# Unread f32 products in the norm gaps and the router, and layer 1's modulation sums moved beside layer 0's feed-forward part

## The chip, the cores and the metric

The kernel runs on one core of a Trainium2 chip. The metric is the device time of one execution in microseconds (us): the median of three runs of the kernel before is 2724.13 us (2723.62 to 2729.8). The engines named below are TensorE (PE, the matrix products; PEld is its weight load), VectorE (DVE), ScalarE (ACT), GpSimd (POOL) and SyncE (SP, which issues the weight loads).

## The reference

Two blocks of two layers each, one after the other, on 256 tokens of width 1024, in float32. Cut to what matters here:

```
# first block, layers l = 0, 1: x (256 tokens) and, in layer 0, ctx (256 more)
mod = silu(c) @ w_mod[l] + b_mod[l]           # six vectors of 1024: shift, scale, gate, twice
h1  = modulate(rmsnorm(h, norm1_g[l]), shift1, scale1)
h   = h + gate1 * (mixing_layer(h1 @ w_in[l]) @ w_out[l])
h2  = modulate(rmsnorm(h, norm2_g[l]), shift2, scale2)
h   = h + gate2 * conv_ffn(h2)

def conv_ffn(h, w_up, conv_w, conv_b, w_down):
    u = h @ w_up                              # 5632 columns
    u = three-tap convolution of u along the tokens
    a, b = split(u, 2)
    return (silu(a) * b) @ w_down

# second block
h = h + even_mix(rmsnorm(h)) ; h = h + swiglu(rmsnorm(h))
h = h + odd_mix(rmsnorm(h))  ; h = h + moe_swiglu(rmsnorm(h))   # a router picks experts
out = rmsnorm(h)
```

The modulation vectors of layer 1 depend on the conditioning input alone, so they can be computed at any time before layer 1's first norm. (Layer 1 needs them for both streams in its first norm, and for the main stream alone elsewhere.)

## The kernel before

Feature rows lie on the 128 partitions and tokens along the free axis, 512 columns in layer 0 (both streams), 256 elsewhere. An f32 product of accuracy is made of three (`mm3`, L519 to L521): high part times high part, low times high, high times low, where the high part is a rounded copy made by ScalarE (`wh`, L488) and the low part the residual made by VectorE (`wl`, L489). Weights come through `load_f` (L514, issued by SP) into a ring of raw tiles `wf`; with three slots in the ring during the feed-forward part, a load waits until the tile three loads earlier is read out.

The stages in order: start and layer 0's mix (to 336 us), the gap of its second norm (to 348), layer 0's feed-forward part (348 to 745), the gap of layer 1's first norm (745 to 752), layer 1's mix (to 951), the second norm and feed-forward part (to 1143), the leave step (1144 to 1153), the second block's first layer (mix to 1358, norm gap, swiglu to 1551), its second layer (norm gap, mix to 1690), the router (1690 to 1697), the experts (to 2708), and the last norm.

A norm (`rstd`, L555) squares tiles of h on ScalarE (L563), adds them on GpSimd (L568) except for the last two, takes column sums with one-column products (L574), a root on ScalarE (L576), a reciprocal on VectorE (L577), and spreads the result over the partitions with `spread` (L605). `modnorm` (L633, L639, L640) then makes the high and low parts `ah`, `al` that the next matmuls need. `first_rstd` (L608) does the same for the very first norm; `leave` (L1151) for the end of the first block, with two norms in one.

The feed-forward part runs in two halves of eleven steps j. In each j two products `up` (a, then b; 24 records each) are followed by the convolution (`conv`: L1092 on ScalarE, L1095 and L1096 on VectorE), the multiply L1070, and the split into `gh`, `gl`. Three ups are started ahead, side by side. After eleven j come the down products.

Layer 1's modulation vectors are made by `mods_v` (L686) on VectorE: a chunk is 384 columns of `w_mod`, loaded in two tiles of 768 KB; for each stream one first product (L698) and seven adding ones (L700), then three one-column products on TensorE (L705) and an add (L708). Six chunks have two streams, ten have one. It is a generator that stops twice in each chunk. `tick` (L712) advances the first unfinished generator in `self.fill`. Before, `fill` held the rest of layer 0's own vectors (`m0`) and then layer 1's (`m1`); it was ticked from places in the mixes, and once in each j of layer 0's feed-forward part, which spread layer 1's sixteen chunks thus: one two-stream chunk in layer 0's mix, five two-stream and six one-stream chunks in layer 0's feed-forward part, four one-stream chunks in layer 1's mix. Instructions are placed by a scheduler that hoists what it can, so the order on an engine isn't that of the text.

Of the kernel before, what the change touches and what calls it, by code (L numbers as in the profile page):

```python
# [16 lines left out]
P = 128  # L17
D = 1024
KT = 8
S = 256  # L20
# [409 lines left out]
class Build:  # L430
# [36 lines left out]
    def load_consts(self, pool, g):  # L467
        n = sum(_CP[x].shape[1] for x in GROUPS[g])
        t = self.mk(pool, [P, n], F32, "c" + g)
        (self.nc.sync if g == "A" else self.nc.gpsimd).dma_start(out=t, in_=self.I["consts" + g])  # L470
        o = 0
        for x in GROUPS[g]:
            w = _CP[x].shape[1]
            self.cs[x] = t[:, o:o + w]
            o += w
        return t
# [75 lines left out]
    def rstd(self, src, kts, n, ones, eps, lead=None):  # L552


        nc = self.nc  # L555
        nt = n // P
        lead = kts - 2 if lead is None else lead
        ps = self.smps()
        r = self.mk(self.wk, [P, 8], F32, "rs", 1)
        total = self.mk(self.wk, [P, n], F32, "ssq", 1) if lead else None  # L560
        for k in range(kts):
            sq = self.t2k()
            nc.scalar.activation(sq[:, :n], src[:, k, :n], AF.Square)  # L563
            if k == (kts - 3 if lead else 1):
                nc.scalar.activation(r[:, 4:5], sq[:, :1], AF.Sqrt)
            if k < lead:
                if k:
                    nc.gpsimd.tensor_tensor(total, total, sq[:, :n], op=OP.add)  # L568
                else:
                    nc.gpsimd.tensor_copy(total, sq[:, :n])  # L570
                continue
            for i, x in enumerate((total, sq) if lead and k == lead else (sq,)):
                for t in range(nt):
                    nc.tensor.matmul(ps[:, t:t + 1], x[:, t * P:t * P + P], ones[:, :1],  # L574
                                     start=k == lead and i + t == 0, stop=k == kts - 1 and t == nt - 1)
        nc.scalar.activation(r[:, :nt], ps[:, :nt], AF.Sqrt, bias=eps)  # L576
        nc.vector.reciprocal(r[:, :nt], r[:, :nt])  # L577
        out = self.smps()
        self.spread(out, r[:, :nt])
        return out  # L580

    def head_rstd(self, sq, n, eps, floor=None):

# [24 lines left out]
    def first_rstd(self, h):  # L608

        nc = self.nc  # L610
        ps = self.smps()
        for k in range(KT):
            sq = self.t2k()
            nc.scalar.activation(sq, h[:, k], AF.Square)
            nc.tensor.matmul(ps, self.c("mean"), sq, start=k == 0, stop=k == KT - 1)
        r = self.mk(self.wk, [P, 512], F32, "ssq", 1)
        nc.scalar.activation(r, ps, AF.Sqrt, bias=self.eps)
        nc.vector.reciprocal(r, r)
        return r
# [292 lines left out]
    def layer_a(self, l):  # L912
# [14 lines left out]
        rs = self.first_rstd(h) if l == 0 else self.rstd(h, KT, N, self.c("mean"), self.eps)  # L927
        if l == 0:
            self.m0 = self.mods(0, ((6, 7, 8, 9), (10, 11, 12, 13), (14, 15)))
            self.m1 = [self.mods_v(1, list(range(6)), 2), self.mods_v(1, list(range(6, 16)), 1)]  # L930
            self.fill = [self.m0] + self.m1

            keep = self.wp, self.wbufs
            sx = ExitStack()
            self.weights(sx, "wpS", (8, 1), 1536, 768)
            start = self.wp, self.wbufs
            m = self.mods(0, MODS_FIRST)
            for _ in MODS_FIRST[0]:
                next(m)
            self.wp, self.wbufs = keep  # L940
            first = [self.load_w(wq[i], KT, P) for i in lead]
            self.wp, self.wbufs = start
            self.drain(m)
            sx.close()
            self.wp, self.wbufs = keep
            self.load_consts(self.bp, "A")
            gs, sh = self.gains(l, 0, "norm1_g", ((0, 3), (3, KT)))
            m = self.m0
        else:
            self.drain(self.m1[0])  # L950
            m = self.m1[1]
            first = [self.load_w(wq[i], KT, P) for i in lead]
            gs, sh = self.gains(l, 0, "norm1_g")
# [103 lines left out]
        gh = self.mk(fp, [P, HT, NX], F32R, "gh")  # L1057
        gl = self.mk(fp, [P, HT, NX], F32R, "gl")

        def up(i):  # L1060
            ps = first.pop(0) if first else self.fm(self.load_w(w_up[i], KT, P), 0, act, 0, NX)
            return self.conv(l, ps, i, ns)

        for half in range(2):
            for f in range(HT):
                j = half * HT + f
                a = up(j)
                nc.scalar.activation(a[:, :NX], a[:, :NX], AF.Silu)
                b = up(NF + j)
                nc.vector.tensor_tensor(b[:, :NX], a[:, :NX], b[:, :NX], op=OP.mult)  # L1070
                if l == 0:
                    self.tick()
                self.split(gh[:, f], gl[:, f], b[:, :NX])
            for ft in range(0, KT, 2):

                ws = [self.load_w(I["w_down"][l, ft + i][:, half * HT:(half + 1) * HT], HT, P) for i in range(2)]
                ps = self.side(ws, (gh, gl), (NX, NX)) if ft == 0 else (self.fm(w, 0, (gh, gl), 0, NX) for w in ws)
                for i, p in enumerate(ps):
                    self.residual(l, ft + i, p, 40, ns)
        self.tap(f"hff{l}", h)  # L1080
        fx.close()
        rs = self.leave() if l else None
# [68 lines left out]
    def leave(self):  # L1151

        nc = self.nc
        ps = self.smps()
        r = self.mk(self.wk, [P, 8], F32, "rs", 1)
        total = self.mk(self.wk, [P, 2 * S], F32, "ssq", 1)
        h = self.h
        for k in range(KT):
            sq = self.t2k()
            hk = self.h[:, k, :S]  # L1160
            nc.scalar.activation(sq[:, :S], hk, AF.Square)
            nc.scalar.activation(sq[:, S:], hk, AF.Square, scale=self.v("final_g", k))
            if k == KT - 3:
                nc.scalar.activation(r[:, 4:5], sq[:, :1], AF.Sqrt)
            if k == 0:
                nc.gpsimd.tensor_copy(total, sq)
            elif k < KT - 2:
                nc.gpsimd.tensor_tensor(total, total, sq, op=OP.add)
            for x in {KT - 2: (total, sq), KT - 1: (sq,)}.get(k, ()):
                for t in range(4):  # L1170
                    nc.tensor.matmul(ps[:, t:t + 1], x[:, t * P:t * P + P], self.c("mean")[:, :1],
                                     start=x is total and t == 0, stop=k == KT - 1 and t == 3)
        r1, r2 = r[:, :2], r[:, 2:4]
        nc.scalar.activation(r1, ps[:, :2], AF.Sqrt, bias=self.eps)
        nc.vector.reciprocal(r1, r1)
        out = self.smps()
        self.spread(out, r1)
        nc.vector.tensor_tensor(r2, r1, r1, op=OP.mult)
        nc.vector.tensor_tensor(r2, r2, ps[:, 2:4], op=OP.mult)
        nc.scalar.activation(r2, r2, AF.Sqrt, bias=self.eps)  # L1180
        nc.vector.reciprocal(r2, r2)
        self.spread(out[:, S:], r2)

        def enter(k):
            nc.vector.scalar_tensor_tensor(self.hb[:, k], h[:, k, :S], self.v("final_g", k), out[:, :S],
                                           op0=OP.mult, op1=OP.mult)

        return out[:, S:], enter
# [427 lines left out]
    def moe(self, sums, copies):  # L1616
# [17 lines left out]
        sel = self.mk(mp, [P, 2, E], F32, "sel")  # L1634
# [4 lines left out]
        rs = self.mk(rp, [P, 2], F32, "rst")  # L1639
# [4 lines left out]
        for tt in range(2):  # L1644
            nc.vector.tensor_copy(lr[:, tt], sums[2 + tt][:, :E])
        nc.vector.reciprocal(rs, rs)

        for tt, sl, ps in copies:
            nc.scalar.activation(th[:, tt, sl], ps, AF.Copy, scale=rs[:, tt:tt + 1])
# [13 lines left out]
        ps = self.smps()  # L1663
# [16 lines left out]
        for tt, sl, pt in copies:  # L1680
            nc.vector.scalar_tensor_tensor(tl[:, tt, sl], pt, rs[:, tt:tt + 1], th[:, tt, sl].bitcast(F32),
                                           op0=OP.mult, op1=OP.subtract)
        cnt = self.mk(mp, [P, 1], F32, "cnt")
        cnti = self.mk(mp, [P, 1], mybir.dt.int32, "cnti")
        nc.vector.tensor_reduce(cnt, cps[:, :E], axis=AX.X, op=OP.max)
# [301 lines left out]
```

## Time and profile before

| | us |
|---|---|
| median of three runs (lowest, highest) | 2724.13 (2723.62, 2729.8) |
| the profiled execution, time | 2726.23 |
| its span | 2724.5 |
| TensorE busy | 2627.1 (96%) |
| VectorE busy | 1969.7 (72%) |
| ScalarE busy | 1566.6 (57%) |
| GpSimd busy | 179.8 (7%) |
[...]

The span is the time from the first to the last instruction of the profiled execution; its time has 1.7 us more around it. [...] A busy share is an average over stages: where TensorE's is near 1, another engine's work costs nothing as long as TensorE never waits for it.

### The profile page before, as it was taken

What the parts mean: (1) busy time and instruction counts of PE and PEld (TensorE: products, weight loads), DVE (VectorE), ACT (ScalarE), POOL (GpSimd) and SP (SyncE); (2) the same over time, 40 slices, a digit from 0 to 9 for tenths busy, and PEclk for the clock granted to TensorE, in tenths of its full rate; (3) what the DMA queues carried; (4) which work ended last, traced back from release to release, by engine and by line L of the source; (5) the groups of instructions that cost most, each with busy time, mean ns of one, the idle gap of its engine ahead of it and who ended that gap; (6) DMA issues with size and microseconds to landing.
All of it is one profiled execution on the core that took longest, in us unless ns stands there. A gap on an engine that the chain in (4) does not pass through costs nothing.

```text
span 2724.5 us, 39224 instructions
## 1 busy us (share of the span) xinstructions
PE 2627.1 (96%) x14886; PEld 2186.7 (80%) x14886; DVE 1969.7 (72%) x2975; ACT 1566.6 (57%) x2363; POOL 179.8 (7%) x212
## 2 busy tenths in 40 slices
PE   7999989999998999999999999999999999999998
PEld 4755678888877799998899988888887787788776
DVE  4245678467366787775665468999989888888886
ACT  4334434234244665564444465877777777777775
POOL 0120200000112200222100100000000000000000
PEclk9999989999999999999999999999999999999999
DMA  7344234344233255530256445899999999999992
GB/s 276 120 140 159 70 114 149 128 147 157 97 126 118 94 181 182 192 123 24 93 178 208 162 166 214 329 366 352 328 356 348 356 339 362 344 360 334 362 347 101
DMA packets 116178, 585.92 MB, mean 215 GB/s; under 512 B 19792, under 2 KB 24416, under 8 KB 71056
## 3 DMA queue, kind: packets, MB, share of 16 engines
q1 hardware_dynamic: 113744, 576.19, 58.8%
q0 software_dynamic: 2240, 7.16, 1.1%
q8 instruction: 119, 1.95, 0.3%
q14 instruction: 75, 0.61, 0.1%
HBM read 581.82 MB, written 1.47 MB: 214 GB/s over the span
## 4 chain that ended last, share of the span: by engine, by line
PE 87%; DVE 5%; DMA 3%; ACT 2%; issue 1%; POOL 0%; SPq 0%; DVEq 0%; ACTq 0%; POOLq 0%
PE mm L519 21%; PE mm L520 21%; PE mm L521 21%; PE dn L520 4%; PE dn L519 4%; PE dn L521 4%; PE sm L166 1%; DVE wl L489 1%; DMA wf<-w_mod 1%; PE sm L1764 1%; DVE m L700 1%; PE sm L772 1%; DMA wf<-w_qkg 1%; PE sm L908 1%; PE sm L1714 1%
## 5 line engine op out<-in xcount | busy, mean ns | idle before, releaser
L489 DVE TENSOR_TENSOR wl<-wf,wh 128x1024 fp32r<-128x1024 f32 (+3 forms) x1178 | 1210.4, 1056 | 357.0 <-ACT wh L488 352.3
L488 ACT CAST wh<-wf 128x1024 fp32r<-128x1024 f32 (+3 forms) x1178 | 1044.2, 912 | 595.3 <-PE mm L520 319.1
L519 PE MATMUL mm<-ah,wh 128*128 128x256 f32 (+1 forms) x1768 | 577.1, 330 | 15.5 <-ACT ah L639 4.0
L521 PE MATMUL mm<-ah,wl 128*128 128x256 f32 (+1 forms) x1768 | 576.6, 327 | 1.7 <-DVE wl L489 1.6
L520 PE MATMUL mm<-al,wh 128*128 128x256 f32 (+1 forms) x1768 | 574.3, 325 | 1.1 <-DVE al L637 1.1
L519 PEld LDWEIGHTS mm<-ah,wh 128*128 128x128 f32 x1768 | 338.9, 193 | 58.3 <-issue 8.5
L521 PEld LDWEIGHTS mm<-ah,wl 128*128 128x128 f32 x1768 | 340.4, 193 | 36.7 <-issue 5.3
L520 PEld LDWEIGHTS mm<-al,wh 128*128 128x128 f32 x1768 | 340.7, 193 | 31.0 <-issue 2.6
L520 PE MATMUL mm<-wl,xh 128*128 128x512 f32 x896 | 357.6, 399 | 2.0 <-DVE wl L489 2.0
L519 PE MATMUL mm<-wh,xh 128*128 128x512 f32 x896 | 355.8, 397 | 0.0
L521 PE MATMUL mm<-wh,xl 128*128 128x512 f32 x896 | 353.3, 395 | 0.0
L520 PEld LDWEIGHTS mm<-wl,xh 128*128 128x128 f32 x896 | 168.4, 188 | 52.0 <-DVE wl L489 13.1
L519 PEld LDWEIGHTS mm<-wh,xh 128*128 128x128 f32 x896 | 168.4, 188 | 38.9
L521 PEld LDWEIGHTS mm<-wh,xl 128*128 128x128 f32 x896 | 168.2, 188 | 37.9
L521 PE MATMUL dn<-wh,eal 128*128 128x512 f32 x448 | 180.7, 403 | 0.0
L520 PE MATMUL dn<-wl,eah 128*128 128x512 f32 x448 | 177.8, 397 | 0.0
L519 PE MATMUL mm<-gh,wh 128*128 128x256 f32 (+1 forms) x528 | 167.9, 318 | 0.0
L521 PE MATMUL mm<-gh,wl 128*128 128x256 f32 (+1 forms) x528 | 167.9, 318 | 0.0
L520 PE MATMUL mm<-gl,wh 128*128 128x256 f32 (+1 forms) x528 | 167.9, 318 | 0.0
L519 PE MATMUL dn<-wh,eah 128*128 128x512 f32 x448 | 157.6, 396 | 0.0
L520 PEld LDWEIGHTS mm<-gl,wh 128*128 128x128 f32 x528 | 99.8, 189 | 8.1
L521 PEld LDWEIGHTS mm<-gh,wl 128*128 128x128 f32 x528 | 99.8, 189 | 8.0
(502 smaller groups left out, 3320.1 us busy)
## 6 DMA issues: line engine op xcount, KB each, us to landing
wf<-moe_wg SPq DMA_DIRECT2D x112, 1024.0 KB, 6.9
wf<-moe_wu SPq DMA_DIRECT2D x112, 1024.0 KB, 6.9
wf<-moe_wd SPq DMA_DIRECT2D x112, 1024.0 KB, 6.3
wf<-w_mod SPq DMA_DIRECT2D x64, 768.0 KB, 4.5
wf<-w_up SPq DMA_DIRECT2D x88, 512.0 KB, 3.5
wf<-w_down SPq DMA_DIRECT2D x32, 704.0 KB, 4.1
wf<-w_qkg SPq DMA_DIRECT2D x30, 512.0 KB, 4.7
wf<-ffn_wg SPq DMA_DIRECT2D x22, 512.0 KB, 4.2
```

The source lines that it names most:

```text
L166: self.nc.tensor.matmul(o, l, r, start=True, stop=True)
L488: nc.scalar.copy(dh, src)
L489: nc.vector.tensor_tensor(dl, src, dh.bitcast(F32), op=OP.subtract)
L519: nc.tensor.matmul(out, lh, rh, start=first, stop=False)
L520: nc.tensor.matmul(out, lh, rl, start=False, stop=False)
L521: nc.tensor.matmul(out, ll, rh, start=False, stop=last)
L700: nc.vector.scalar_tensor_tensor(acc[s], w3[:, k - k0], c, acc[s], op0=OP.mult, op1=OP.add)
L772: nc.tensor.transpose(pt[:, k * P:k * P + P], pr[:, k * P:k * P + P], self.c("ident"))
L908: nc.tensor.matmul(ops[rows, s * S:s * S + S], nav[:, t0 + k, hh * 64:hh * 64 + 64], PT[par][:, k].rearrange("p a b -> p (a b)"), start=k ...
L1714: nc.tensor.matmul(ps[:, m * S:m * S + S], src[:, tt, k * P:k * P + P], G[:, tt, e0:e0 + 2], start=tt == 0, stop=tt == 1)
L1764: nc.tensor.transpose(ps[:, j * P:j * P + P], s[:, j * P:j * P + P], self.c("ident"))
```

## The change

Two things are changed. First, a new function `warm(n, w)` issues n plain f32 products of 128x256 whose results nobody reads: `w` (the identity by default, else a small tile that has just been made) times the first 256 columns of the constants `com`, into a buffer of the small accumulators. Each norm gets three at its front, two after the one-column products with the last squares as `w`, and three after the spread with the reciprocal as `w`; `first_rstd` gets four, `leave` 3, 2, 1 and 5, the router three and three. Second, `fill` holds only `m0` in layer 0's mix; before layer 0's feed-forward part it is set to `m1`, and `tick` is called before every `up` of that part (44 times) in place of once per j (22 times). All sixteen chunks now lie in layer 0's feed-forward part: six two-stream and five one-stream chunks in its first half, five one-stream chunks in the second.

```
+    def warm(self, n, w=None):
+        w = self.c("ident") if w is None else w
+        ps = self.smps()
+        for _ in range(n):
+            self.nc.tensor.matmul(ps[:w.shape[1], :S], w, self.com[:, :S], start=True, stop=True)
...
 def rstd:
+        self.warm(3)
         ps = self.smps()
...
+        self.warm(2, sq[:, :P])
         nc.scalar.activation(r[:, :nt], ps[:, :nt], AF.Sqrt, bias=eps)
         nc.vector.reciprocal(r[:, :nt], r[:, :nt])
         out = self.smps()
         self.spread(out, r[:, :nt])
+        self.warm(3, r[:, :nt])
...
 def first_rstd (after the mean products):
+        self.warm(4)
...
 def layer_a:
-            self.fill = [self.m0] + self.m1
+            self.fill = [self.m0]
...
+        if l == 0:
+            self.fill = list(self.m1)
+
         def up(i):
+            if l == 0:
+                self.tick()
             ps = first.pop(0) if first else self.fm(self.load_w(w_up[i], KT, P), 0, act, 0, NX)
...
                 nc.vector.tensor_tensor(b[:, :NX], a[:, :NX], b[:, :NX], op=OP.mult)
-                if l == 0:
-                    self.tick()
...
 def leave:
+        self.warm(3)
...
+        self.warm(2, sq[:, :P])
...
         self.spread(out, r1)
+        self.warm(1, r1)
...
         self.spread(out[:, S:], r2)
+        self.warm(5, r2)
...
 router of moe:
         nc.vector.reciprocal(rs, rs)
+        self.warm(3, rs)
...
+        self.warm(3, sel[:, 0])
         cnt = self.mk(mp, [P, 1], F32, "cnt")
```

On VectorE, in the first half of layer 0's feed-forward part, before, from behind the multiply of one j on: `wl` are the residuals of up weights, `m_0` and `m_1` the accumulators of a modulation chunk, the second operand of a `t2k` row the accumulator of an up.

```order
L489 TENSOR_TENSOR wl_2961<-wf_2958,wh_2960 128x512
L489 TENSOR_TENSOR wl_2965<-wf_2958,wh_2964 128x512
L489 TENSOR_TENSOR gl_2767<-t2k_2931,gh_2766 128x512
L489 TENSOR_TENSOR wl_3001<-wf_2998,wh_3000 128x512
L489 TENSOR_TENSOR wl_3005<-wf_2998,wh_3004 128x512
L708 SCALAR_TENSOR_TENSOR mod_12_90<-sm_3038,V_61 128x3 x2
L489 TENSOR_TENSOR wl_3052<-wf_3049,wh_3051 128x512
L489 TENSOR_TENSOR wl_3056<-wf_3049,wh_3055 128x512
L489 TENSOR_TENSOR wl_3092<-wf_3089,wh_3091 128x512
L489 TENSOR_TENSOR wl_3096<-wf_3089,wh_3095 128x512
L1095 SCALAR_TENSOR_TENSOR t2k_2993<-mm_2968,V_61,t2k_2993 128x2x255
L698 TENSOR_SCALAR m_1_14_92<-wf_3129,csf_83 128x384
```

And after the change, from the residual of the gated tile of one j to the next j's first weight residual (L491 is the residual, L711 and L713 the modulation products, L1111 and L1112 the conv steps, L1088 the multiply):

```order
L491 TENSOR_TENSOR gl_2754<-t2k_2865,gh_2753 128x512
L491 TENSOR_TENSOR wl_2895<-wf_2892,wh_2894 128x512
L491 TENSOR_TENSOR wl_2899<-wf_2892,wh_2898 128x512
L721 SCALAR_TENSOR_TENSOR mod_12_90<-sm_2932,V_61 128x3 x2
L491 TENSOR_TENSOR wl_2944<-wf_2941,wh_2943 128x512
L491 TENSOR_TENSOR wl_2948<-wf_2941,wh_2947 128x512
L711 TENSOR_SCALAR m_1_14_92<-wf_2983,csf_83 128x384
L711 TENSOR_SCALAR m_0_13_91<-wf_2983,csf_83 128x384
...
L1111 SCALAR_TENSOR_TENSOR t2k_2976<-mm_2951,V_61,t2k_2976 128x2x255
...
L1112 SCALAR_TENSOR_TENSOR t2k_2976<-mm_2951,V_61,t2k_2976 128x2x255
...
L1088 TENSOR_TENSOR t2k_2976<-t2k_2927,t2k_2976 128x512
L491 TENSOR_TENSOR wl_3006<-wf_3003,wh_3005 128x512
```

Before, the residuals of four ups stand ahead of the next conv steps and modulation products. After, the two ups' residuals of a j stand ahead of a whole chunk and both conv steps of that j, and the next residual comes behind the multiply.

On TensorE, at the gap of layer 1's first norm, before: the last down product, the one-column products, the spread, the mix's first product.

```order
L521 MATMUL mm_5414<-gh_2766,wl_5375 128x512
L574 MATMUL sm_5461<-ccom_65,ssq_5463 128x1 x4
L574 MATMUL sm_5461<-ccom_65,t2k_5483 128x1 x4
L574 MATMUL sm_5461<-ccom_65,t2k_5493 128x1 x4
L605 MATMUL sm_5501<-ccom_65,rs_5462 128x128 x4
L519 MATMUL mm_5606<-ah_5459,wh_5508 128x256
```

And after the change (L592 is `warm`'s product):

```order
L523 MATMUL mm_5498<-gh_2753,wl_5459 128x512
L592 MATMUL sm_5545<-ccom_65 128x256 x3
L577 MATMUL sm_5549<-ccom_65,ssq_5551 128x1 x4
L577 MATMUL sm_5549<-ccom_65,t2k_5571 128x1 x4
L577 MATMUL sm_5549<-ccom_65,t2k_5581 128x1 x4
L592 MATMUL sm_5587<-ccom_65,t2k_5581 128x256 x2
L617 MATMUL sm_5592<-ccom_65,rs_5550 128x128 x4
L592 MATMUL sm_5597<-ccom_65,rs_5550 4x256 x3
L521 MATMUL mm_5701<-ah_5543,wh_5603 128x256
```

Three unread products now stand ahead of the one-column products, two between these and the spread, and three between the spread and the next useful product. The other norms read alike, but the leave step and the norm ahead of the second block's second layer keep two of the front three, and the second block's swiglu norm none: the scheduler moved the others far ahead into the stage before, or behind the first products of the stage that follows another norm.

## Rows read from the trace of the kernel before

**Rows 1.** Windows by stage: stretch, length, busy us (instructions) by engine, PEclk, DMA.

```profile
350.00:400.00 50.00, 44.61 (x175) 35.14 (x174) 42.59 (x84) 20.70 (x36) 0.00 (x0) 0.88 0.26 87
550.00:745.00 195.00, 195.00 (x855) 157.44 (x854) 117.00 (x189) 73.41 (x115) 8.05 (x7) 1.00 0.40 135
330.00:350.00 20.00, 15.29 (x64) 13.04 (x63) 14.05 (x29) 8.57 (x18) 9.53 (x9) 0.72 0.62 178
744.00:770.00 26.00, 24.21 (x122) 20.67 (x121) 18.61 (x42) 13.79 (x28) 5.77 (x8) 0.87 0.34 105
940.00:960.00 20.00, 16.64 (x127) 16.08 (x126) 14.35 (x30) 11.26 (x25) 4.63 (x6) 0.92 0.57 198
1143.00:1155.00 12.00, 8.41 (x50) 6.92 (x50) 6.38 (x16) 4.46 (x10) 5.44 (x8) 0.70 0.97 273
1350.00:1366.00 16.00, 11.83 (x86) 10.85 (x85) 13.24 (x22) 9.71 (x21) 11.72 (x11) 0.90 0.92 327
1547.00:1560.00 13.00, 11.20 (x73) 10.75 (x72) 9.02 (x21) 5.14 (x12) 4.42 (x6) 0.77 0.70 257
1690.00:1710.00 20.00, 16.28 (x84) 14.36 (x83) 17.75 (x57) 11.77 (x23) 0.00 (x0) 0.83 0.19 58
2700.00:2724.00 24.00, 13.19 (x72) 11.07 (x70) 9.05 (x18) 5.80 (x13) 0.00 (x0) 0.73 0.15 47
```

**Rows 2.** VectorE, layer 0's mix: start, duration, engine, line, operation, idle before.

```profile
250.54 7.49 DVE L700 SCALAR_TENSOR_TENSOR m<-wf,csf,m 128x384 f32<-128x384 f32 x14
```

**Rows 3.** VectorE's timeline in layer 1's mix.

```profile
782.24 0.42 DVE L698 TENSOR_SCALAR m<-wf,csf 128x384 f32<-128x384 f32 x1 [4.54 <-DMA wf<-w_mod]
...
838.49 0.42 DVE L698 TENSOR_SCALAR m<-wf,csf 128x384 f32<-128x384 f32 x1 [4.38 <-DMA wf<-w_mod]
...
845.34 1.27 DVE L700 SCALAR_TENSOR_TENSOR m<-wf,csf,m 128x384 f32<-128x384 f32 x2 [2.67 <-DMA wf<-w_mod]
```

**Rows 4.** TensorE's timeline in layer 0's feed-forward part.

```profile
360.23 0.40 PE L519 MATMUL mm<-ah,wh 128*128 128x512 f32 x1
...
365.85 0.40 PE L519 MATMUL mm<-ah,wh 128*128 128x512 f32 x1
...
494.11 0.39 PE L519 MATMUL mm<-gh,wh 128*128 128x512 f32 x1
```

**Rows 5.** VectorE groups, 350 to 744: shapes, count, busy us, mean ns, idle.

```profile
L700 DVE SCALAR_TENSOR_TENSOR m<-wf,csf,m 128x384 f32<-128x384 f32 x111 | 64.8, 611 | 1.7 <-DMA wf<-w_mod 1.4
L489 DVE TENSOR_TENSOR wl<-wf,wh 128x512 fp32r<-128x512 f32 x87 | 58.3, 685 | 38.3 <-ACT wh L488 38.3
```

**Rows 6.** ScalarE's and VectorE's timelines behind an up, and a later multiply.

```profile
382.58 0.78 ACT L1092 ACTIVATE t2k<-mm,V 128x512 f32<-128x512 f32 x1 [4.97 <-PE mm L521]
383.39 0.75 DVE L1095 SCALAR_TENSOR_TENSOR t2k<-mm,V,t2k 128x510 f32<-128x510 f32 x1 [2.04 <-ACT t2k L1092]
...
385.77 0.68 DVE L1070 TENSOR_TENSOR t2k<-t2k,t2k 128x512 f32<-128x512 f32 x1
...
437.72 0.68 DVE L1070 TENSOR_TENSOR t2k<-t2k,t2k 128x512 f32<-128x512 f32 x1
```

**Rows 7.** TensorE's groups, 1180 to 1186: a plain f32 product of 128x256.

```profile
L183 PE MATMUL sm<-wa,w2a 128*128 128x256 f32 x12 | 2.9, 388 | 0.0
```

**Rows 8.** TensorE's timeline in the gap of layer 0's second norm.

```profile
338.93 1.87 PE L574 MATMUL sm<-ccom,ssq 128*128 128x1 f32 x8 [2.56 <-POOL ssq L568]
340.66 3.55 PE L574 MATMUL sm<-ccom,t2k 128*128 128x1 f32 x16
344.78 2.08 PE L605 MATMUL sm<-ccom,rs 128*128 128x128 f32 x8 [0.57 <-DVE rs L577]
348.44 0.80 PE L519 MATMUL mm<-ah,wh 128*128 128x512 f32 x1 [1.58 <-ACT ah L639]
```

**Rows 9.** TensorE's timeline in the gap of layer 1's first norm.

```profile
744.97 0.95 PE L574 MATMUL sm<-ccom,ssq 128*128 128x1 f32 x8
745.78 2.10 PE L574 MATMUL sm<-ccom,t2k 128*128 128x1 f32 x16
```

More of the change, by code (lines that the diff above doesn't have):

```diff
@@ L469, in load_consts @@
         t = self.mk(pool, [P, n], F32, "c" + g)
+        if g == "com":
+            self.com = t
         (self.nc.sync if g == "A" else self.nc.gpsimd).dma_start(out=t, in_=self.I["consts" + g])
@@ L557, in rstd @@
         lead = kts - 2 if lead is None else lead
+        self.warm(3)
         ps = self.smps()
@@ L575, in rstd @@
                                      start=k == lead and i + t == 0, stop=k == kts - 1 and t == nt - 1)
+        self.warm(2, sq[:, :P])
         nc.scalar.activation(r[:, :nt], ps[:, :nt], AF.Sqrt, bias=eps)
@@ L579, in rstd, with warm @@
         self.spread(out, r[:, :nt])
+        self.warm(3, r[:, :nt])
         return out
+    def warm(self, n, w=None):
+        w = self.c("ident") if w is None else w
+        ps = self.smps()
+        for _ in range(n):
+            self.nc.tensor.matmul(ps[:w.shape[1], :S], w, self.com[:, :S], start=True, stop=True)
     def head_rstd(self, sq, n, eps, floor=None):
@@ L615, in first_rstd @@
             nc.tensor.matmul(ps, self.c("mean"), sq, start=k == 0, stop=k == KT - 1)
+        self.warm(4)
         r = self.mk(self.wk, [P, 512], F32, "ssq", 1)
@@ L930, in layer_a @@
             self.m1 = [self.mods_v(1, list(range(6)), 2), self.mods_v(1, list(range(6, 16)), 1)]
-            self.fill = [self.m0] + self.m1
+            self.fill = [self.m0]
             keep = self.wp, self.wbufs
@@ L1058, in layer_a @@
         gl = self.mk(fp, [P, HT, NX], F32R, "gl")
+        if l == 0:
+            self.fill = list(self.m1)
         def up(i):
+            if l == 0:
+                self.tick()
             ps = first.pop(0) if first else self.fm(self.load_w(w_up[i], KT, P), 0, act, 0, NX)
@@ L1070, in layer_a @@
                 nc.vector.tensor_tensor(b[:, :NX], a[:, :NX], b[:, :NX], op=OP.mult)
-                if l == 0:
-                    self.tick()
                 self.split(gh[:, f], gl[:, f], b[:, :NX])
@@ L1153, in leave @@
         nc = self.nc
+        self.warm(3)
         ps = self.smps()
@@ L1173, in leave @@
         r1, r2 = r[:, :2], r[:, 2:4]
+        self.warm(2, sq[:, :P])
         nc.scalar.activation(r1, ps[:, :2], AF.Sqrt, bias=self.eps)
@@ L1177, in leave @@
         self.spread(out, r1)
+        self.warm(1, r1)
         nc.vector.tensor_tensor(r2, r1, r1, op=OP.mult)
@@ L1182, in leave @@
         self.spread(out[:, S:], r2)
+        self.warm(5, r2)
         def enter(k):
@@ L1646, in moe @@
         nc.vector.reciprocal(rs, rs)
+        self.warm(3, rs)
         for tt, sl, ps in copies:
@@ L1682, in moe @@
                                            op0=OP.mult, op1=OP.subtract)
+        self.warm(3, sel[:, 0])
         cnt = self.mk(mp, [P, 1], F32, "cnt")
```

## The prediction

> **What bounds the kernel now.** I read the page first, then the windows by stage, then inside the stages that the change touches the groups of instructions, the timelines and the waits. TensorE is busy for 96% of the span, so nearly everything else lies beside it, and the question at each place is only whether TensorE waits longer or shorter there, or runs at a lower clock. The windows [rows 1] show three kinds of stretch. In the rest of layer 0's feed-forward part (550 to 745) TensorE is busy for 195.00 of 195 us at a clock of 1.00, with VectorE busy for 117: room for extra VectorE work. In its first half (350 to 400) it is busy for 44.61 of 50 at a clock of 0.88, and VectorE for 42.59: no room. In the eight windows around the norms, the leave step, the router and the end, the clock is 0.70 to 0.92, and TensorE is busy for 117.1 of 151 us (sums over the eight rows).
>
> **Part 1: the modulation chunks that leave the mixes.** A two-stream chunk is 16 VectorE products of 128x384 and 12 one-column TensorE records. Layer 0's mix had one: fourteen adding products, 7.49 us in one block [rows 2], after two first ones of 0.42 like that in rows 3: some 8.2 us, behind which VectorE's mix work queued. TensorE had other matmuls for much of that time, so I take half, -4 us, with ends 0 and -8. Layer 1's mix had four one-stream chunks. Their products waited for their own weights on VectorE's queue, 4.54 us before the product at 782.24, then 4.38 and 2.67 [rows 3], and whatever VectorE had behind them waited as well. Behind the first nothing stands that TensorE needs before about 784 us, so I give it 2 us; the last two stand directly ahead of the score work, so I give these 6 of their 7.05 us, and 2 us for TensorE's own column sums. Sum -10 us. The ends are -2 (only the sums) and -14 (every wait shown and the sums).
>
> **Part 2: all sixteen chunks in the feed-forward part.** This term decides. One up product is 24 TensorE records, 5.62 us from 360.23 to 365.85 [rows 4]. For each pair of ups (one j) VectorE does sixteen modulation products, of 0.611 us by themselves and 7.49 / 14 = 0.535 when they follow each other, four weight residuals of 0.685 [rows 5], four conv steps of 0.75 [rows 6], a multiply and a residual of the gated tile. With the same overlap of 0.08 taken off each: 16 x 0.53 + 4 x 0.61 + 4 x 0.67 + 2 x 0.61 = 14.8 us, against 2 x 5.62 + 1.2 = 12.4 us on TensorE. Before, a two-stream chunk stood in about every second j, so that VectorE's average was near TensorE's. Now six j in succession carry a two-stream chunk, and the other five a one-stream chunk of half that size. Over the eleven j this gives VectorE some 27 us more: 3.2 chunks of 8.2, since six two-stream and five one-stream chunks (8.5 units) stand where five and about half a one stood.
>
> More than the sum, the order counts. After the change, the four residuals of a j come in VectorE's order behind conv b and the multiply of the j before (the order rows of the change show it); before, they ran up to eight ahead. So in the two-stream stretch TensorE has exactly two ups to do and then waits for a loop: ScalarE's first tap, which starts at 382.58, the conv steps, the multiply at 385.77 [rows 6], and the first residual, 0.61 us each for the last two when the overlap of 0.08 is taken off: 385.77 + 1.22 - 382.58 = 4.4 us from the end of one up to the start of the next. A j then costs 11.24 + 1.2 + 4.4 = 16.8 us.
>
> Where that leads: the second j's multiply stood at 385.77. The fourth up's residual now has about ten more products of the second chunk ahead of it, 5 us. Then come four loops, 67.2 us, where these four j took 51.95 (385.77 to 437.72 [rows 6]): +15. After an idle stretch of this size TensorE's clock has fallen before: the window 350 to 400 has 0.88 [rows 1], that is 12 of its 50 us at the low level. I put two such falls into the four loops, at 3.4 us each (the 12 us are two falls and a rest, and half of 6.8 is lost): +7. From there to the end of the ups, five one-stream j at TensorE's pace, 0.6 + 5 x 11.84 = 59.8 us, where before it was 494.11 - 437.72 = 56.4 [rows 4, 6], since TensorE then was some way behind VectorE: +3. Sum 5 + 15 + 7 + 3 = +30 us. The lower end: only VectorE's work counts, and of the 27 us some 19 are made up in VectorE's idle time: +8. The upper end: a fall in each loop, and the fourth up 10 us late: +42. In the second half five one-stream chunks, 5 x 4.1 = 21 us of VectorE work, lie beside a TensorE that is busy all the time: nothing, and if that cover were gone, at most these 21.
>
> **Part 3: the unread products.** A plain f32 product of 128x256 stands in the trace once: 12 records, busy for 2.9 us in all with the last one's end, so six products at about 0.47 us each [rows 7]. Eight per norm are 3.8 us of TensorE. Their cost: the front three (1.4) are free where the one-column products wait for GpSimd's total, 2.56 us at 338.93 [rows 8]. Where there is no such wait [rows 9], here and in three other gaps, they delay the gap by what stands there, three or two products: about 4.6 in all. The two behind the one-column products take 0.94 us where the root and the reciprocal leave TensorE 0.57 [rows 8]: 0.37 x 8 = 3.0. The three behind the spread fit into 1.58 us of waiting [rows 8], elsewhere with a little over: 1 in all, the router's with it. They have only two or four weight columns each. Sum 4.6 + 3.0 + 1, about +8.5 us. The four behind first_rstd stand where TensorE waits for modulation weights: nothing.
>
> The gain is clock. [...] The eight gap windows of rows 1 give 11.2 + 6.8 + 3.2 + 7.2 + 3.2 + 6.0 + 6.8 + 13.0 = 57 us at the low level. Half of that, times TensorE's busy share of 117/151, is 22 us, the most that can come back. The same sixteen one-column records show the two levels: 3.55 us [rows 8] and 2.10 [rows 9]. But the 24 records from 338.93 on ran one behind the other to 344.2, and the clock did not rise: that the engine was occupied was not enough. With a wider operand it may be. I take half of the 22: -11 + 8.5, about -3 us. Ends: -14 (all comes back) and +20 (nothing does, and most of the products run at the low level themselves).
>
> [...]
>
> **Sum.** -4 - 10 + 30 - 3 = +13 us. The profiled execution took 2726.23 us with a span of 2724.5; the median shown is 2724.13, 2 us less. I add the sum to the median: 2737 us.
>
> **Rivals.** First, the lead of the residuals is not lost as the order suggests, and only VectorE's work counts: +8 in place of +30. For it: in the window 350 to 400 TensorE is busy for 44.61 of 50 us beside a nearly full VectorE. Against it: the residuals stand behind conv b in an order that is kept. -4 - 10 + 8 - 3 = -9: 2715 us, the other side. It decides from the point where the feed-forward term falls under about +9.
>
> Second, the products hold the clock in every gap (-14), and the loops run at full clock too (30 - 7 = +23): -4 - 10 + 23 - 14 = -5, so 2719 us, no change that can be told. For it: 57 us at the low level. Against it: the 24 records. [...]
>
> Third, the products don't change the clock and only delay: +12 (between 8.5 and 20) in place of -3. -4 - 10 + 30 + 12 = +28: 2752 us. For it: the same 24 records. Against it: 256 columns are more than one.
>
> **How the numbers follow.** A difference under 0.3%, 8 us, is no change that a measurement of this kernel tells. Forecast 0.40, rivals 0.20, 0.24 and 0.16. Faster: 0.16 of the first rival and 0.05 of the second, 0.21. Slower: 0.30 of the forecast, 0.16 of the third, 0.02 of the second, 0.48. Same: the rest, 0.31. The range goes from the first rival's time to the third's, a little wider at each end: 2713 to 2753; the forecast's own, with its feed-forward term between +15 and +41, is 2722 to 2748.
>
> **What would show it.** In the profile after: layer 0's first-half ups end near 520 instead of 494, with four to six waits of TensorE of some 3 to 5 us for a VectorE residual between 380 and 470, and a window 400 to 450 with TensorE under 45 of 50 us. If TensorE is busy there for 49 or more, part 2 is wrong. In layer 1's mix VectorE has no wait for modulation weights, and the stretch from norm 1 to norm 2 is shorter by 10 us. In the gap windows a clock of 0.9 or more where it was 0.70 to 0.87 says that the second rival holds; a clock as before, with gaps longer by 1 us each, the third.

## The result and the profile after

The changed kernel is slower: a median of 2749.89 us (2746.01 to 2750.29, four runs) against 2726.97 us for the kernel before in the runs beside it, a ratio of 1.0079 with a 95% interval of 1.0056 to 1.0101. The forecast was 2737 us, range 2713 to 2753. The profiled execution took 2746.01 us with a span of 2744.2.

I cut both traces at the same instructions (the first one-column product of each norm, the first useful product behind it, the first down product of each half) and took the lengths:

```
stage                                        before    after   difference
start to layer 0's second norm                338.9    336.5     -2.4
its gap                                         9.5      9.3     -0.2
layer 0, first-half ups                       145.7    169.2    +23.5
first down products, second-half ups          189.2    188.6     -0.6
second down products                           61.7     62.9     +1.2
gap of layer 1's first norm                     6.7      5.9     -0.8
layer 1's mix                                 201.2    192.7     -8.5
gap of layer 1's second norm                    4.5      4.1     -0.4
layer 1's feed-forward part                   186.7    185.9     -0.8
gap of the leave step                           7.0     11.3     +4.3
second block, first mix                       210.2    209.7     -0.5
gap of the swiglu norm                          4.4      7.5     +3.1
swiglu                                        185.0    189.1     +4.1
gap of the second mix's norm, second mix      143.3    142.4     -0.8
router, experts                              1014.5   1014.2     -0.3
last norm                                      15.9     14.8     -1.2
```

The chain of waits of the changed kernel between two j of the two-stream stretch (start, duration, engine, what):

```profile
405.59 0.79 ACT t2k L1108
406.40 0.75 DVE t2k L1111
407.15 0.53 DVE m L713
407.68 0.66 DVE t2k L1112
408.33 0.53 DVE m L713
408.86 0.60 DVE t2k L1088
409.46 0.61 DVE wl L491
410.08 0.04 issue
410.12 0.69 PE mm L523
```

From the end of one up to the product of the next that needs the residual 4.5 us pass, in first tap, conv steps, two modulation products between them, multiply and residual. This is the loop of [rows 6] with the residual at its end. TensorE is not idle for all of it: the first four of the next up's 24 products and the chunk's twelve one-column products (its column sums) run in that time, and it is busy for 2.81 of 4.50 us. The window, and what TensorE waited for between 346 and 515 us (us in total, times, longest):

```profile
405.60:410.10 4.50, 2.81 (x16) 1.79 (x14) 4.46 (x9) 2.40 (x4) 0.00 (x0) 1.00 0.07 10
```

```profile
PE sm L718 <- DVE m L713: 10.0, 7, 6.6
PE mm L521 <- ACT wh L490: 7.4, 5, 3.4
PE mm L523 <- DVE wl L491: 2.7, 4, 1.6
```

The multiplies on VectorE's timeline, and TensorE's first down product:

```profile
389.77 0.68 DVE L1088 TENSOR_TENSOR t2k<-t2k,t2k 128x512 f32<-128x512 f32 x1
408.78 0.68 DVE L1088 TENSOR_TENSOR t2k<-t2k,t2k 128x512 f32<-128x512 f32 x1
425.46 0.69 DVE L1088 TENSOR_TENSOR t2k<-t2k,t2k 128x512 f32<-128x512 f32 x1
442.14 0.69 DVE L1088 TENSOR_TENSOR t2k<-t2k,t2k 128x512 f32<-128x512 f32 x1
458.17 0.69 DVE L1088 TENSOR_TENSOR t2k<-t2k,t2k 128x512 f32<-128x512 f32 x1
```

```profile
514.98 0.40 PE L521 MATMUL mm<-gh,wh 128*128 128x512 f32 x1
```

They answer to 385.77 and 437.72 [rows 6] and to 494.11 [rows 4]: 19.0, 16.7, 16.7 and 16.0 us apart, 68.4 us where four j took 51.95.

The windows of the changed kernel, at the places of [rows 1] (stretch, length, busy time by engine with instruction counts, then TensorE's granted clock, the DMA share and GB/s). In short stretches of the kernel before the clock reads 0.50 (338.93 to 352.50, 373.10 to 379.90 us) or 1.00 (353 to 373 us), so a mean between the two says how much of a window ran at 0.50, the low level:

```profile
326.00:346.00 20.00, 18.85 (x84) 14.49 (x83) 15.22 (x32) 9.20 (x19) 10.34 (x10) 0.83 0.69 213
345.00:395.00 50.00, 35.06 (x142) 27.81 (x141) 45.67 (x97) 16.17 (x30) 0.00 (x0) 0.77 0.29 95
512.00:706.00 194.00, 194.00 (x847) 156.50 (x846) 122.06 (x194) 70.33 (x108) 0.00 (x0) 1.00 0.40 137
765.00:791.00 26.00, 25.96 (x145) 22.02 (x144) 19.30 (x42) 13.81 (x28) 5.79 (x8) 1.00 0.38 121
952.00:972.00 20.00, 20.00 (x156) 18.60 (x155) 15.20 (x32) 11.48 (x26) 4.84 (x6) 1.00 0.57 199
1154.00:1170.00 16.00, 15.25 (x74) 10.30 (x72) 8.22 (x21) 4.90 (x12) 4.63 (x6) 0.79 0.88 253
1368.00:1384.00 16.00, 12.52 (x66) 9.96 (x66) 9.89 (x18) 7.33 (x16) 15.19 (x14) 0.79 0.65 247
1569.00:1582.00 13.00, 13.00 (x98) 11.69 (x97) 8.21 (x21) 5.15 (x12) 4.42 (x6) 1.00 0.64 233
1711.00:1731.00 20.00, 18.11 (x101) 13.55 (x100) 18.86 (x59) 13.03 (x24) 0.00 (x0) 1.00 0.23 76
2721.00:2744.00 23.00, 13.51 (x82) 10.66 (x80) 7.67 (x17) 6.11 (x13) 0.00 (x0) 0.87 0.15 49
```

In the first half TensorE is busy for 35.06 of 50 us where it was 44.61. Four gaps (layer 1's two norms, the second mix's norm, the router) now run at a clock of 1.00, where they had 0.87, 0.92, 0.77 and 0.83; layer 0's second norm has 0.83 for 0.72, the end 0.87 for 0.73. The leave step and the swiglu norm stay low: 0.79 each. For the swiglu norm that is no change: its window in [rows 1], with 0.90, ends inside the low stretch, and 16 us that take in all of it have 0.79 before, too:

```profile
1354.00:1370.00 16.00, 11.91 (x76) 11.14 (x75) 14.01 (x26) 8.92 (x20) 14.42 (x13) 0.79 0.69 252
```

The timeline of the leave gap, VectorE before, then VectorE and TensorE after:

```profile
1149.60 0.48 DVE L1185 SCALAR_TENSOR_TENSOR hb<-h,V,sm 128x256 f32<-128x256 f32 x1 [1.32 <-PE sm L605]
1150.11 0.48 DVE L633 SCALAR_TENSOR_TENSOR t2k<-hb,V,sm 128x256 f32<-128x256 f32 x1
1150.51 2.50 DVE L489 TENSOR_TENSOR wl<-wf,wh 128x512 fp32r<-128x512 f32 x4
```

```profile
1158.48 1.20 PE L592 MATMUL sm<-ccom,t2k 128*128 128x256 f32 x2
...
1160.47 1.01 PE L592 MATMUL sm<-ccom,rs 128*2 128x256 f32 x2
1161.41 1.23 PE L617 MATMUL sm<-ccom,rs 128*128 128x128 f32 x4
...
1162.68 0.48 DVE L1205 SCALAR_TENSOR_TENSOR hb<-h,V,sm 128x256 f32<-128x256 f32 x1 [2.57 <-PE sm L617]
1163.07 2.49 DVE L491 TENSOR_TENSOR wl<-wf,wh 128x512 fp32r<-128x512 f32 x4
1165.48 0.47 DVE L646 SCALAR_TENSOR_TENSOR t2k<-hb,V,sm 128x256 f32<-128x256 f32 x1
```

Two things add up. The unread products delay the second spread (it starts 6.3 us behind the gap's first one-column product, before 4.3: 1161.41 - 1155.12 against 1148.34 - 1144.07). And four weight residuals now stand ahead of the norm's next step in VectorE's order, where they stood behind it: 2.4 us more. TensorE in the swiglu norm's gap after the change:

```profile
1376.15 0.97 PE L577 MATMUL sm<-ccom,ssq 128*128 128x1 f32 x4 [3.42 <-POOL ssq L571]
...
1378.68 2.05 PE L592 MATMUL sm<-ccom,t2k 128*128 128x256 f32 x4
...
1381.52 2.20 PE L592 MATMUL sm<-ccom,rs 128*2 128x256 f32 x6
```

The wait for GpSimd's total is there still (2.37 before), since the scheduler moved the front three far ahead of it, and the unread products run at the low level (0.50 from 1378.68 to 1380.73): two take 2.05 us, where six took 2.9 [rows 7]. Not all of the +3.1 is theirs: mods_only below has +1.6 here without any, its gap at a clock of 0.61 (1371.9 to 1384.9), where it is 0.70 before (1359.3 to 1370.7).

### The profile page after: what moved, and what is told of

Read it like the earlier page. It is cut to its first block, busy times and chain, and to the rows that moved or that the text cites. A ratio compares the mean times of both kernels' runs of the same rounds, so it can differ in the third digit from the quotient of the medians.

```text
span 2744.2 us, 39490 instructions
## 1 busy us (share of the span) xinstructions
PE 2654.9 (97%) x15024; PEld 2196.9 (80%) x15024; DVE 1969.5 (72%) x2975; ACT 1567.4 (57%) x2363; POOL 179.1 (7%) x212
## 4 chain that ended last, share of the span: by engine, by line
PE 90%; DVE 4%; ACT 2%; DMA 2%; issue 1%; POOL 1%; SPq 0%; DVEq 0%; POOLq 0%; ACTq 0%
PE mm L521 22%; PE mm L522 22%; PE mm L523 21%; PE dn L521 4%; PE dn L522 4%; PE dn L523 4%; PE sm L166 1%; PE sm L592 1%; DVE wl L491 1%; PE sm L1786 1%; PE sm L785 1%; PE sm L921 1%; ACT wh L490 1%; PE sm L1736 1%; PE mm L914 1%
## 5 line engine op out<-in xcount | busy, mean ns | idle before, releaser
L491 DVE TENSOR_TENSOR wl<-wf,wh 128x1024 fp32r<-128x1024 f32 (+3 forms) x1178 | 1211.2, 1057 | 391.7 <-ACT wh L490 386.0
L521 PEld LDWEIGHTS mm<-ah,wh 128*128 128x128 f32 x1768 | 333.3, 190 | 57.0 <-ACT wh L490 11.6
L523 PEld LDWEIGHTS mm<-ah,wl 128*128 128x128 f32 x1768 | 334.5, 189 | 38.1 <-DVE wl L491 6.4
L521 PEld LDWEIGHTS mm<-gh,wh 128*128 128x128 f32 x528 | 99.2, 188 | 8.1
```

What stands on the lines that cost most here:

```text
L491: nc.vector.tensor_tensor(dl, src, dh.bitcast(F32), op=OP.subtract)
L521: nc.tensor.matmul(out, lh, rh, start=first, stop=False)
L523: nc.tensor.matmul(out, ll, rh, start=False, stop=last)
```

## The experiments

Each lists the differences of the stages against before as in the table above.

**mods_only: the chunks alone.** Before, with the change's second part:

```
-            self.fill = [self.m0] + self.m1
+            self.fill = [self.m0]
...
+        if l == 0:
+            self.fill = list(self.m1)
         def up(i):
+            if l == 0:
+                self.tick()
...
-                if l == 0:
-                    self.tick()
```

> The chunks moved as in the change, no unread products. Theory (TensorE waits out a loop behind conv b because the residuals lost their lead): the three stage terms of the changed kernel stay without the products, layer 0's mix -2.4, first-half ups +23.5, layer 1's mix -8.5, the gaps as before: about +12.6 us on before, multiplies of the two-stream j 16.7 us apart. Rival (the products ahead of the feed-forward part, through the clock or the delay, made part of it): first-half ups under +15, sum near 0.

2747.09 us, ratio 1.0082 (1.0066 to 1.0099). First-half ups +25.9, layer 1's mix -9.2, start -2.0, multiplies 16.7 us apart behind a first loop of 19.0, leave gap 0.0; the swiglu stage is +4.6 here too. The gaps are not all as before: layer 0's second norm -2.3, the swiglu norm +1.6. The theory's three stage terms hold, and the loss is there without the products; over this kernel they give nothing that can be told (1.0079 with them, 1.0082 without).

**products_only: the products alone.** The changed kernel with `fill` and `tick` put back.

> The unread products as in the change, the chunks where they were. Theory (they hold the clock in some gaps and delay others): gaps and what lies right behind them +4 us against before, and +4 more if the second block's swiglu weights again go at 118 ns a record instead of 113. Rival 1 (activity releases the clock, so they gain): -5 us or better. Rival 2 (the gap losses of the changed kernel came from the moved chunks): 0.

2716.38 us, ratio 0.9967 (0.9948 to 0.9986): faster, so the theory's +4 is wrong and rival 1 holds. First-half ups -6.8, layer 1's mix -6.0 with all four chunks still in it, second mix -2.6, layer 1's first ups -1.6; leave gap +4.1, swiglu norm's gap +3.7, second down products +1.3 (the front three of the next norm). The gain lies behind the gaps, not in them, and the clock goes with it: in the first-half ups it is 0.98 (345.4 to 484.3), before 0.94 (348.4 to 494.1), in layer 1's mix 0.98 for 0.94. In the gaps it is 1.00 in layer 1's second norm (937 to 949), the second mix's norm (1540 to 1552) and the router (1680 to 1700), but 0.89 in the leave step (1128 to 1144) and 0.66 in the swiglu norm (1347.5 to 1362.6).

**ahead: the lead given back.** mods_only, with the weights of a later up loaded and split before each up of the first half:

```
+        seq = [c for f in range(HT) for c in (f, NF + f)][3:]
+        ready = []
         def up(i):
+            if l == 0 and i % NF < HT:
+                if seq and i:
+                    ready.append(self.load_w(w_up[seq.pop(0)], KT, P))
+                self.tick()
+                ps = first.pop(0) if first else self.fm(ready.pop(0), 0, act, 0, NX)
...
```

> As mods_only, but in the first half of layer 0's feed-forward part each call of up first loads and splits the weights of a later up, so that VectorE's residuals stand ahead of the chunk's products by one j. Theory (order): the multiplies of the two-stream j come 14.8 to 15.2 us apart, VectorE's own work, and the first-half ups lose 10 us less than in mods_only. Rival (something else in the loop binds, as the weight loads behind the ring of three): 16.7 us apart as before.

2736.75 us, ratio 1.0048 (1.0030 to 1.0066). First-half ups +5.0 in place of +25.9. Its multiplies on VectorE:

```profile
402.78 0.68 DVE L1084 TENSOR_TENSOR t2k<-t2k,t2k 128x512 f32<-128x512 f32 x1
417.23 0.69 DVE L1084 TENSOR_TENSOR t2k<-t2k,t2k 128x512 f32<-128x512 f32 x1
431.67 0.68 DVE L1084 TENSOR_TENSOR t2k<-t2k,t2k 128x512 f32<-128x512 f32 x1
```

14.45 us apart, less than the 14.8 to 15.2 expected: VectorE's own work, since it is busy in every moment of the four loops,

```profile
388.35:446.12 57.77, 54.44 (x241) 43.74 (x241) 57.77 (x113) 20.14 (x32) 0.00 (x0) 0.94 0.56 183
```

and nearly none of that work was taken away: 131 modulation products lie in these ups, 133 in mods_only. So 21.0 of the 25.9 us were the order, more than the 10 expected: 10.6 in the four loops, 6.0 up to the second j's multiply, where the wait for the fourth up went, and 4.3 behind the sixth. Not all of it reaches the kernel's time. The second half is 4.6 us longer, layer 1's mix gains only 5.6, and between the medians of mods_only and this run lie 10.3 us: more than half of mods_only's loss, not all of it.

**late: the chunks beside the second half.** No products, `fill` as in the change; one tick per j in the first half, one per up in the second.

```
+            if l == 0 and i % NF >= NF // 2:
+                self.tick()
...
+                if l == 0 and half == 0:
+                    self.tick()
```

> No unread products. Ticks once per j in the first half as before, and at every up in the second half of layer 0's feed-forward part, so that ten and a half chunks lie beside TensorE's busy second half and none in layer 1's mix nor in layer 0's. Theory: first-half ups as before, second half longer by at most the column sums, 4 to 6 us, mixes -11: about -6 us on before. Rival (the second half has no room either): +8 or more.

2728.77 us, ratio 1.0009 (0.9995 to 1.0023): no change. First-half ups -0.3 and second half +4.6 as the theory has it; layer 1's mix -5.9, but the start +1.6 instead of a gain, and 2.4 us more in three gaps. The chunk that left layer 0's mix bought nothing.

**front_three and tail_only: which products hold the clock.** products_only with the front products alone, and with those behind the spread and in the router alone.

> products_only with the front three of each norm and of the leave step alone (identity as weights, 128 columns), and first_rstd's four. Theory A (products with full weights hold the clock through the one-column products, as layer 1's first norm of products_only shows): most of the -10 us stays, -6 to -10 on before, since the delays behind the one-column products are gone. Theory B (the products behind the spread, just ahead of the useful matmuls, hold it): within 3 us of before.

> products_only with the products behind the spread and in the router alone (two or four weight columns). Theory A: within 3 us of before, clock in the gap windows as before. Theory B: -6 to -10.

One time each: 2719.90 and 2718.85 us, against 2728.13 for the median of before beside them; no interval. Layer 1's second norm and the router, first in front_three, then in tail_only:

```profile
942.00:956.00 14.00, 13.13 (x88) 12.30 (x87) 10.68 (x25) 7.90 (x20) 1.50 (x2) 0.88 0.36 114
1685.00:1705.00 20.00, 16.27 (x82) 14.09 (x82) 18.06 (x56) 12.65 (x23) 0.00 (x0) 0.83 0.22 69
```

```profile
945.00:958.00 13.00, 11.33 (x86) 9.79 (x85) 11.02 (x25) 8.25 (x20) 1.52 (x2) 1.00 0.39 123
1686.00:1706.00 20.00, 18.39 (x98) 13.64 (x98) 18.32 (x59) 13.90 (x25) 0.00 (x0) 1.00 0.28 98
```

Neither theory alone. With the products behind the spread (two weight columns in that norm) and those in the router (three with two, three with eight) the clock stays at 1.00 in these two places; the router has no front products in front_three, so its 0.83 is that of before. The norm ahead of the second mix has 0.88 in tail_only (1545 to 1559) and 0.86 in front_three (1544 to 1556), and 1.00 only with all the products (products_only, 1540 to 1552). tail_only also shows that the leave gap's loss (+4.0) belongs to the products behind its spreads; front_three has -0.1 there.

**sel: the products without three places.** products_only without those of the leave step, the swiglu norm and the last norm.

> products_only without the products of the leave step, of the second block's swiglu norm and of the last norm. Theory (they hold the clock in some gaps, and in these three only delay): leave gap back from 11.1 to 7.0, swiglu norm's from 8.1 to about 4.5, the end from 16.6 to 16: about 8 us under products_only, 2707. Rival (the losses there come with the clock's timing and turn up elsewhere): as products_only, 2716.

2711.09 us, ratio 0.9933 (0.9914 to 0.9952). Leave gap +0.2 in place of +4.1, last norm -1.1. Of the expected 8 us 5.3 came between the medians, and the two intervals overlap. The swiglu norm's gap is still +2.0. The leave gap is 3.9 us shorter than in products_only, but the second block's first mix, right behind it, is 5.8 us longer (+4.8 against -1.1), and the clock around the gap is 0.68 (1128 to 1140) against 0.89 (1128 to 1144). There the rival holds, and that the leave step is better off without its products is not shown.

**sel_ahead: both.** sel with the edit of ahead, the chunks where they were before.

> sel with the later up's weights loaded and split before each up of the first half, as in ahead, the chunks where they were before. Theory (lead of the residuals): the first-half ups fall from 139 to about 134, TensorE's own work there, 4 us under sel. Rival (with the clock held nothing is left to gain): as sel.

2706.73 us, ratio 0.9921 (0.9902 to 0.9940), the fastest of all. First-half ups 133.3, from 139.0 in sel and 145.7 before: the theory's figure. Behind the leave step the first mix is +2.5.

**after_again and after_ahead.** The changed kernel once more, and with the edit of ahead.

> The changed kernel once more, unaltered, to see which stage terms repeat. Theory: first-half ups +23.5, leave gap +4.3 and the swiglu norm's gap +3 repeat within 1 us; the swiglu stage of the second block at 118 ns a record in place of 113 (+4) repeats too if it belongs to the program. Rival: that stage is back at 185 us, a matter of the single execution.

2746.27 us, one time. Ups +23.6, leave gap +4.4, swiglu norm's gap +3.0: these repeat. The swiglu stage does not: 184.5 us. A window of ten us there, in the changed kernel's first profile and in this one:

```profile
1424.00:1434.00 10.00, 10.00 (x87) 10.00 (x86) 5.75 (x8) 5.26 (x8) 0.00 (x0) 1.00 0.56 190
```

```profile
1424.00:1434.00 10.00, 10.00 (x91) 10.00 (x90) 6.18 (x8) 4.50 (x7) 0.00 (x0) 1.00 0.64 203
```

Both at a clock of 1.00, 87 records against 91. So the slow pace doesn't belong to the program; mods_only (+4.6) and after_ahead (+4.1) have it as well, ahead and late don't.

> The changed kernel with one more edit, the later up's weights loaded and split before each up of the first half. Theory (the whole loss is the residuals' lost lead): the two-stream multiplies 14.4 us apart, first-half ups near 150 in place of 169, second half +5 since the chunks run on into it: about 14 us under the changed kernel, 2733 to 2736. Rival (with the products the clock in the loops matters more): under 8 us.

2725.91 us, ratio to before 0.9985 (0.9971 to 1.0000); 24 us under the changed kernel's median, 20 under after_again beside it, 15 between the two profiles, where 14 was expected. First-half ups +3.2, multiplies 14.4 us apart (409.93, 424.37, 438.81), second half +5.5. One edit to the order takes the loss against before away. It also lets the products count: with this order the kernel has 1.0048 without them (ahead) and 0.9985 with them, where the changed kernel and mods_only could not be told apart. (Its profile, at 2731.16 us, is the slowest of its ten runs, so the stages show little of this.)

## Why the prediction held, point by point

- **The order of VectorE, +30.** The mechanism held, shown by mods_only and ahead. By its parts: the second j came 6.6 us late (389.77 - 345.8 from the first useful product against 385.77 - 348.4), 5 was forecast; the four loops took 68.4, which is +16.5, where 15 + 7 was forecast; the five one-stream j and the end took 56.8, +0.4, where +3 was. 23.5 in all. That the later loops took 16.7 us, where 16.8 was worked out, is in part luck. The 16.8 has no fall of the clock in it, but the clock fell in each of the four: it is 0.50 from 389.8 to 396.6, 410.3 to 413.6, 427.4 to 430.7 and 444.5 to 447.7. TensorE's products behind the residual show what that costs:

```profile
410.12 0.69 PE L523 MATMUL mm<-ah,wl 128*128 128x512 f32 x1 [0.37 <-DVE wl L491]
...
413.60 0.43 PE L522 MATMUL mm<-al,wh 128*128 128x512 f32 x1
```

Eight products start in these 3.48 us, where they would need 1.87 at the 5.62 us for 24 of [rows 4]: 1.6 us in each of the last three loops, and about as much in the first, some 6 in all. So the 7 us for the falls were near. The term that was too large is TensorE's share behind the wait: the column sums (1.2) and four of the 48 products (0.9) run inside the wait, as the window 405.6 to 410.1 shows. For the same reason the sign did not come as written: TensorE's waits for the residual are four with 2.7 us in all, not four to six of 3 to 5, because it waits ahead of them, in its own order, 10.0 us for the column sums of VectorE's chunk. The window 400 to 450 has TensorE busy for 44.82 of 50 us, as the sign wanted.
- **Layer 1's mix, -10.** -8.5, and -9.2 without the products; but -6.6 in after_again, which is the same program, and -5.6 and -5.9 in ahead and late, where no chunk is left there either. That VectorE's waits for modulation weights went is sure (14.0 us before between 752 and 951, none after); that this is all of it isn't, since the products alone gave -6.0 there with the chunks in place, and the two don't add.
- **Layer 0's mix, -4.** -2.4, but -2.8 in products_only, where the chunk stayed, and +1.6 in late, where it went. The chunk's share isn't shown; with it and without it the stage varies alike.
- **The products, -3.** This is the step that failed, in what it was made of: alone they are worth -9 us (0.9967), over the moved chunks nothing that can be told. In the changed kernel the stages apart from the three above are +7.2, of which 4.1 is the swiglu stage's pace, which comes and goes. The 57 us of the prediction stand in the trace: within its eight windows the clock reads 0.50 for 11.07 + 6.83 + 3.25 + 7.11 + 3.07 + 5.92 + 6.82 + 12.80 = 56.9 us. The clock did come back in four of the gaps (1.00), as the second rival had it; my doubt, drawn from the one-column records, did not carry over to products of 256 columns there, and in the leave step and the swiglu norm it is 0.79. But I priced delays on TensorE alone. In the leave step they also let four weight residuals pass the norm on VectorE; in the swiglu norm the front three were moved far ahead, so that they cover no wait there, and the rest ran at the low level (0.51 from 1376.15 to 1382): together +7.4, of which 1.6, in the swiglu norm's gap, stands in mods_only without any product. (The router's second three have eight weight columns, not two or four as the prediction says.)
- **The sum.** +13 forecast, +19.7 between the two profiled spans, and the ratio's interval is +15 to +28 us: the forecast was too low. 2749.89 lies 2 us outside of the forecast's own 2722 to 2748, and inside the range because the range reaches to the third rival, 2752; that rival's account, a clock as before, is not what the four windows show, so this part of the agreement is luck. The products gain 0.33% alone and nothing on top of the moved chunks: in the first-half ups, where they gained 6.8 us, the loops bring the clock down in any case, to 0.90 with the products (345.8 to 515.0) and 0.88 without (mods_only, 344.2 to 515.8).

Open: why a stage paces at 113 or 118 ns a record (from start to start in the swiglu, before and after) at a clock of 1.00; and why the first mixes vary by 2 to 4 us between kernels that are alike there, layer 1's even between two executions of one program (-8.5 and -6.6).

## What to carry to other kernels

When work is moved beside a busy engine, compare the order, not the sums: a residual that a waiting engine needs must keep its lead over the work that is added, and issuing its load one step earlier was worth 21 us of 26 in the stage itself and 10 us of 19 in the kernel's time. Unread products between stages held the clock at 1.00 in four gaps here, not in the other two (0.79 each), and alone they paid in the stage behind (-6.8 us in the first-half ups); but each gap is a case of its own: look what they push on the other engines (four residuals in the leave step), and judge a gap together with the stage behind it, since leaving the leave step's products out made its gap 3.9 us shorter and the mix behind it 5.8 us longer.

## What the runs showed of the hardware

With unread products of two weight columns (in the router of eight, too) and 256 data columns TensorE's clock stayed at 1.00 through two gaps of tail_only, layer 1's second norm and the router, where before it was 0.92 and 0.83; ahead of the second mix it was 0.88 with them. Through 24 one-column products back to back, 338.93 to 344.2 us before, it had stayed at 0.50. In each loop of the changed kernel it fell to 0.50 (410.3 to 413.6 in one, behind 4.50 us of which TensorE was busy for 2.81), and eight products took 3.48 us in place of 1.87, worked out from the 5.62 us for 24 of [rows 4]. The same matmuls ran at 87 or 91 records in 10 us, both at a clock of 1.00, in two executions of one program.
